# The order of a weight unit's raw halves, and a later, pinned split of the unit two ahead

## The chip, the cores and the metric

One core of a Trainium2 chip runs the whole kernel. The metric is device microseconds of one execution. ACT is ScalarE, DVE is VectorE, POOL is GpSimd, SP is SyncE, which issues nearly all transfers; PE is TensorE.

## The reference

A decoder block on 1024 tokens of width 1024, in fp32: two token mixers side by side, then a squared-ReLU MLP.

```
xn = rmsnorm(x, norm1_g)
qa, ka, va, qr, kr, vr, gr, gate_a, gate_b = columns of xn @ w_in          # 1024 x 12800
o_a = dilated sliding-window attention(qa, ka, va)   # 12 heads of 128, three windows
o_r = chunkwise retention(qr, kr, vr), group norm, times silu(gr)          # 4 heads
y = sigmoid(gate_a) * (o_a @ w_proj_a) + sigmoid(gate_b) * (o_r @ w_proj_b)
x = x + y @ w_out
x = x + square(relu(rmsnorm(x, norm2_g) @ w_up)) @ w_down                  # 1024 x 4096, 4096 x 1024
```

## The kernel before

Every fp32 matrix product is made of three products of rounded parts: each operand is split into a high part (`wh`, `xh`, a copy on ACT to the rounded type) and a low part (`wl`, `xl`, the difference, on DVE). The helper is `split`, lines 351 (ACT) and 352 (DVE); a wide split of 128x1024 is one instruction on each.

Large products go by a Strassen scheme of seven products N1 to N7 instead of eight. A *unit* is 256 output columns of a weight: 1024 x 256 numbers, which arrive as two raw halves of 512 KB, `s[0]` with quarters (x22, x21) and `s[1]` with (x11, x12). From them four pieces are split:

- A: (x11, x12) as it came, for N1 and N2
- D: x22 as it came, for N4; after it four sums (`sums`, line 151, DVE) rewrite both halves in place
- B: the sums in the half of (x11, x12), for N6 and N3
- C: the sums in the half of (x22, x21), for N5 and N7

There are two places for A, two for B, one for C and two half places for D. The raw halves rotate through four places, two to a unit. `Weights` holds the planning: `steps` is the list of splits in order; `pump` carries out the next step when the pieces it overwrites are given back (`before`, from `claim`) and its raw half is loaded; `load` (line 207) issues the next transfer in order of `src` when its place is free. `free` gives a piece back: after N2, N7, N3 and N4. So every transfer and split is written into the program at a point that follows from these rules.

That is the order in which the program is traced. On PE this order is kept. On ACT, DVE and SP a list scheduler of the compiler sets the final order from its own estimates of when each instruction is ready, unless `tc.keep_in_program_order(ins)` pins an instruction behind the one traced before it on its engine. [...]

The order of products around the change, `strassen_order` (line 287): after N1 and N2 of units 0 and 1, unit j brings

```python
order += [(j, "N6"), (j, "N5")] + ([] if late else [(j + 2, "N1")]) + [(j, "N7")]
order += [(j, "N3")]
order += [(j + 2, "N2")] if not late else ...
order += [(j, "N4")]
```

so N1 and N2 of a unit run two units ahead of the rest. A product is 12 matmuls into one bank. `N1`'s negated result goes to a bank in which N6, N7 and N4 accumulate (bank b, tile `ms`, line 419); N6 is copied out (tile `u`, line 424) before N7 may add to the bank, and N5 (line 427) before N3 may add to its own. Lines 429 and 434 finish the results of N7 and N3 on DVE.

The scheme is used twice: in the input stage ("in", 24 units: gates, retention's q and k, and gr), beside which the attention runs; and in the MLP's first half ("up", 16 units). In up, `result` applies relu (line 1219) and square (line 1220), forms the sums of line 1227 that the second half needs, and `put_operand` splits each of seven operands per unit into a tile `hs` (four buffers) and stores it to DRAM (`h_d<-hs`, line 1237). The second half ("dn", w_down) is another Strassen scheme, whose operands come back from DRAM (`xh<-h_d`, `xl<-h_d`, line 1253) and whose weights come as quarters through the same four raw places (sums at line 183).

Of the kernel before, what the change touches and what calls it, by code (L numbers as in the profile page):

```python
# [12 lines left out]
AF = mybir.ActivationFunctionType  # L13
# [6 lines left out]
D = 1024  # L20
# [8 lines left out]
C = 128  # L29
# [8 lines left out]
class Weights:  # L38
# [10 lines left out]
    A, B, C, D = (0, 1), (2, 3), 5, 4  # L49
# [75 lines left out]
    def add_units(self, tag, srcs):  # L125

        base = len(self.src)
        kept = {}
        for s in srcs:
            self.place += [(len(self.src) + i - base) % (self.RAW + 1) for i in range(2)]  # L130
            self.src += [s[0], s[1]]

        def piece(key, buf, r, cols, then=None):
            def step():
                if isinstance(buf, tuple):
                    if not kept:
                        kept["D"] = self.buffer(buf[0])
                    h, l = (x[:, 512 * buf[1]:512 * buf[1] + 512] for x in kept["D"])
                else:
                    h, l = self.buffer(buf)  # L140
                self.split(h, l, self.raw[r][:, cols])
                self.units[key] = h, l
                if then:
                    then()

            self.steps.append((self.claim(buf, key), r, step))

        def sums(r):
            (x22, x21), (x11, x12) = ((self.raw[i][:, 0:512], self.raw[i][:, 512:1024]) for i in (r, r + 1))
            for x, y in ((x22, x21), (x21, x11), (x11, x22), (x12, x11)):  # L150
                self.nc.vector.tensor_tensor(x, x, y, op=OP.add)  # L151

        both = slice(0, 1024)
        for j in range(-1, len(srcs)):
            if j + 1 < len(srcs):
                r = base + 2 * (j + 1)
                piece((tag, j + 1, "A"), self.A[(j + 1) % 2], r + 1, both)
            if j >= 0:
                r = base + 2 * j
                piece((tag, j, "D"), (self.D, j % 2), r, slice(0, 512), lambda r=r: sums(r))  # L160
                piece((tag, j, "B"), self.B[j % 2], r + 1, both, lambda r=r: self.used.add(r + 1))
                piece((tag, j, "C"), self.C, r, both, lambda r=r: self.used.add(r))
        m = len(srcs)
        self.cycle = (0, 1, self.B[m % 2], self.C, self.D, self.B[(m - 1) % 2])
        self.turn = 0
# [135 lines left out]
def hybrid_block(ctx: ExitStack, tc: tile.TileContext, a: dict, out: bass.AP):  # L301
    nc = tc.nc
# [44 lines left out]
    def bcast_row(src):  # L347
        return bass.AP(tensor=src.tensor, offset=src.offset, ap=[[0, P], [1, D]])

    def split(dst_h, dst_l, src):  # L350
        nc.scalar.activation(dst_h, src, AF.Copy)  # L351
        nc.vector.tensor_tensor(dst_l, src, dst_h.bitcast(F), op=OP.subtract)  # L352

    half = const.tile([P, 4], F, name="half")
# [13 lines left out]
    def halves():  # L368
        return (slice(0, 512), slice(512, 1024))


    W = Weights(nc, rawp, wp, split)
    heads = [(slot, g) for slot in range(SLOTS) for g in (1, 2, 0)]
    for u in range(4):
# [134 lines left out]
    with ExitStack() as ph:  # L509
# [11 lines left out]
        def put_transposed(xn, n, q):  # L521
            t = TILES[n]
            pt = tr.tile([P, 4, P], F, name="tr")
            for i in range(4):
                k = 4 * q + i
                nc.tensor.transpose(pt[:, i, :], xn[:, k * P:(k + 1) * P], ident)
            if q == 0 and t >= 4:
                x01[t] = [px.tile([P, 4, P], R, name=f"x01{i}") for i in "hl"]
                split(*x01[t], pt)
                for i in range(2):  # L530
                    nc.sync.dma_start(x01_d[i, :, :, cut(t)], x01[t][i].bitcast(F))
            else:
                split(*(x[:, :, cut(t)] for x in XS[q, t // 4]), pt)
            x = kept[q, t // 4] = px.tile([P, 4, P], F, name=f"x{q}{t // 4}", bufs=1 if t >= 4 else 2)
            nc.scalar.activation(x, pt, AF.Copy)
            if q == 1 and t >= 4:
                x = dict(kept)
                differences(t, x, (("N5", (0, 0), (0, 1), OP.subtract), ("N7", (0, 1), (1, 1), OP.subtract)))
                pipe.at(1, lambda: differences(t, x, (("N6", (1, 1), (0, 0), OP.add),
                                                      ("N4", (1, 0), (1, 1), OP.subtract))))  # L540
# [22 lines left out]
        lo, hi = halves()  # L563
# [631 lines left out]
    with ExitStack() as ph:  # L1195
# [47 lines left out]
        sums = {}  # L1243
# [190 lines left out]
```

## Time and profile before

| | |
|---|---|
| median of 3 runs | 2262.45 us (2255.77 to 2265.8) |
| the profiled execution | 2260.28 us, its span 2258.5 us |
| mean granted clock of PE | 0.993 |
| the input stage with the attention | about 407 to 985 us |
| up | about 1600 to 1940 us |
| down | from there to the end |

How to read the rows: "start, length, engine, line, operation, out<-in" is a row of the timeline, with what ended the engine's idle time before it in brackets. "out<-in" goes by the names of tiles. Rows of waits are "engine, line <- what it waited for: total us, times, longest". Rows by windows give the stretch, its length, busy us and instruction count of PE, PE's weight load, DVE, ACT and POOL, the granted clock, the share of the DMA engines and GB/s.

### The profile page before, as it was taken

The page shows a single profiled execution, that of the slowest core. Times are in us where ns is not written, and L with a number is a line of the kernel's source. Part 1 is how long each engine was busy: PE and PEld are TensorE (multiplying, and loading weights), DVE is VectorE, ACT ScalarE, POOL GpSimd, SP SyncE. Part 2 cuts the span into 40 slices and gives each one's busy share as a digit, 9 for nine tenths or more (in the row PEclk, how much of TensorE's full clock was granted, in tenths as well). Part 3 has the DMA queues.
Part 4 walks back from the last instruction along what each step waited for, and adds up shares of the span by engine and source line. Part 5 has one row for each costly group of instructions (what it writes and reads, how often), then busy time and mean ns, then how long its engine had stood idle before and what let it go on. Part 6 is the DMA issues. An engine that isn't in the chain of part 4 may idle for free.

```text
span 2258.5 us, 28527 instructions
## 1 busy us (share of the span) xinstructions
PE 2189.5 (97%) x10064; PEld 1794.3 (79%) x10064; DVE 1432.1 (63%) x2543; ACT 1103.3 (49%) x1934; POOL 194.1 (9%) x180
## 2 busy tenths in 40 slices
PE   8999999999999999989999999999999999899998
PEld 6788788888888887878888788888787777688887
DVE  6766676455655666557867741544867778676863
ACT  6433453577744477545545522113666667522210
POOL 3314453000000000000000000000000000000002
PEclk9999999999999999999999999999999999999999
DMA  6443534454555445455333583553388779966657
GB/s 197 131 126 112 150 93 123 154 161 146 172 151 166 153 151 162 127 177 153 119 89 115 165 284 126 187 177 134 109 232 229 231 225 284 313 243 249 244 221 172
DMA packets 346559, 392.77 MB, mean 174 GB/s; under 512 B 34737, under 2 KB 271921, under 8 KB 346162
## 3 DMA queue, kind: packets, MB, share of 16 engines
q1 hardware_dynamic: 344114, 386.77, 54.7%
q0 software_dynamic: 2304, 4.20, 1.3%
q8 instruction: 79, 1.29, 0.2%
q14 instruction: 62, 0.51, 0.1%
HBM read 252.39 MB, written 138.51 MB: 173 GB/s over the span
## 4 chain that ended last, share of the span: by engine, by line
PE 71%; DVE 8%; DMA 8%; ACT 6%; issue 4%; POOL 3%; SPq 0%; POOLq 0%; ACTq 0%; DVEq 0%
PE mm L254 41%; PE ms L254 24%; DMA raw<-in_w_up 2%; ACT wh L351 2%; DVE wl L352 2%; DMA h_d<-hs 2%; PE tr L787 1%; PE tr L806 1%; DVE raw L151 1%; DVE hs L352 1%; DMA xl<-h_d 1%; POOL x L547 1%; DMA raw<-in_w_att_q 1%; DVE xl L352 1%; PE tr L645 1%
## 5 line engine op out<-in xcount | busy, mean ns | idle before, releaser
L352 DVE TENSOR_TENSOR wl<-raw,wh 128x1024 fp32r<-128x1024 f32 (+1 forms) x292 | 332.4, 1139 | 231.5 <-ACT wh L351 229.8
L351 ACT ACTIVATE wh<-raw 128x1024 fp32r<-128x1024 f32 (+1 forms) x292 | 287.1, 986 | 321.3 <-PE ms L254 110.5
L254 PE MATMUL mm<-xh,wh 128*128 128x512 f32 x896 | 346.3, 410 | 0.0
L254 PE MATMUL mm<-xl,wh 128*128 128x512 f32 x896 | 329.0, 390 | 1.7 <-DVE xl L352 1.7
L254 PE MATMUL mm<-xh,wl 128*128 128x512 f32 x768 | 300.7, 392 | 0.0
L254 PE MATMUL mm<-wh,xh 128*128 128x512 f32 x736 | 297.8, 405 | 2.3 <-ACT ms L1273 2.3
L254 PE MATMUL mm<-wh,xl 128*128 128x512 f32 x736 | 289.3, 393 | 4.0 <-DMA xl<-h_d 4.0
L254 PE MATMUL mm<-wl,xh 128*128 128x512 f32 x736 | 288.0, 391 | 0.0
L254 PE MATMUL ms<-xh,wh 128*128 128x512 f32 x544 | 228.2, 419 | 15.3 <-ACT u L424 13.4
L254 PE MATMUL ms<-xl,wh 128*128 128x512 f32 x544 | 213.6, 393 | 0.7 <-DVE xl L352 0.7
L254 PE MATMUL ms<-xh,wl 128*128 128x512 f32 x544 | 213.6, 393 | 0.0
L254 PEld LDWEIGHTS mm<-xh,wh 128*128 128x128 f32 x896 | 168.9, 189 | 32.5 <-ACT u L427 0.4
L254 PEld LDWEIGHTS mm<-xl,wh 128*128 128x128 f32 x896 | 169.0, 189 | 31.6 <-DVE xl L352 2.1
L254 PEld LDWEIGHTS mm<-xh,wl 128*128 128x128 f32 x768 | 144.3, 188 | 31.4
L254 PEld LDWEIGHTS mm<-wh,xl 128*128 128x128 f32 x736 | 138.9, 189 | 35.3 <-DMA xl<-h_d 4.9
L254 PEld LDWEIGHTS mm<-wh,xh 128*128 128x128 f32 x736 | 139.2, 189 | 28.8 <-ACT ms L1273 3.2
L254 PEld LDWEIGHTS mm<-wl,xh 128*128 128x128 f32 x736 | 139.5, 189 | 26.0
L254 PE MATMUL ms<-wh,xh 128*128 128x512 f32 x336 | 137.1, 408 | 6.7 <-DVE c L700 4.4
L254 PEld LDWEIGHTS ms<-xh,wh 128*128 128x128 f32 x544 | 102.9, 189 | 40.8 <-ACT u L424 18.5
L254 PE MATMUL ms<-wh,xl 128*128 128x512 f32 x336 | 132.8, 395 | 2.5 <-DVE xl L352 2.5
L254 PE MATMUL ms<-wl,xh 128*128 128x512 f32 x336 | 132.3, 394 | 1.0 <-DVE ss L365 0.8
L254 PEld LDWEIGHTS ms<-xh,wl 128*128 128x128 f32 x544 | 102.7, 189 | 22.5
(282 smaller groups left out, 3809.9 us busy)
## 6 DMA issues: line engine op xcount, KB each, us to landing
h_d<-hs SPq DMA_DIRECT2D x112, 512.0 KB, 5.6
xh<-h_d SPq DMA_DIRECT2D x32, 896.0 KB, 4.9
xl<-h_d SPq DMA_DIRECT2D x32, 896.0 KB, 6.9
raw<-in_w_att_q SPq DMA_DIRECT2D x48, 512.0 KB, 4.3
raw<-in_w_up SPq DMA_DIRECT2D x32, 512.0 KB, 5.0
raw<-in_w_down SPq DMA_DIRECT2D x32, 512.0 KB, 5.2
qk_d<-T SPq DMA_DIRECT2D x48, 256.0 KB, 3.5
raw<-in_w_gate_q SPq DMA_DIRECT2D x16, 512.0 KB, 4.5
```

Of the source, the lines that this page charges most:

```text
L151: self.nc.vector.tensor_tensor(x, x, y, op=OP.add)
L254: self.nc.tensor.matmul(ps, x, y, start=start, stop=stop, skip_group_check=not first)
L351: nc.scalar.activation(dst_h, src, AF.Copy)
L352: nc.vector.tensor_tensor(dst_l, src, dst_h.bitcast(F), op=OP.subtract)
L547: nc.gpsimd.tensor_tensor(x[v], x[v], x[u], op=op)
L645: nc.tensor.transpose(pt[:, i, :], c[:, i * P:(i + 1) * P], ident)
L787: nc.tensor.matmul(sp[:, :w], q[:, e * P:(e + 1) * P], k[:, k0 * P:k0 * P + w], start=True, stop=True)
L806: nc.tensor.matmul(po[:, :DH], st["t"][:, j * P:(j + 1) * P], v[:, k0 + j, :], start=(j == 0), stop=(j == nk - 1))
```

## The change

The two raw halves of a unit change places in the list of transfers: first (x11, x12), then (x22, x21). Everything that names them follows: A and B read the first, D and C the second, so B gives back the first place and C the second. The step of A of unit j + 1 now also waits until A of unit j is given back, which is after N2 of unit j (before, it waited for N2 of unit j - 1 alone, and came right after C). In up, from unit 2 on, the ACT instruction of A's split is pinned in program order. Nothing changes in the arithmetic, the sizes or the number of transfers.

```diff
-            self.src += [s[0], s[1]]
+            self.src += [s[1], s[0]]
 
-        def piece(key, buf, r, cols, then=None):
+        def piece(key, buf, r, cols, then=None, after=(), pinned=False):
...
-                self.split(h, l, self.raw[r][:, cols])
+                self.split(h, l, self.raw[r][:, cols], pinned)
...
-            self.steps.append((self.claim(buf, key), r, step))
+            self.steps.append((self.claim(buf, key).union(after), r, step))
 
         def sums(r):
-            (x22, x21), (x11, x12) = ((self.raw[i][:, 0:512], self.raw[i][:, 512:1024]) for i in (r, r + 1))
+            (x11, x12), (x22, x21) = ((self.raw[i][:, 0:512], self.raw[i][:, 512:1024]) for i in (r, r + 1))
...
-                piece((tag, j + 1, "A"), self.A[(j + 1) % 2], r + 1, both)
+                piece((tag, j + 1, "A"), self.A[(j + 1) % 2], r, both,
+                      after=((tag, j, "A"),) if j > 0 else (), pinned=tag == "up" and j > 0)
             if j >= 0:
                 r = base + 2 * j
-                piece((tag, j, "D"), (self.D, j % 2), r, slice(0, 512), lambda r=r: sums(r))
-                piece((tag, j, "B"), self.B[j % 2], r + 1, both, lambda r=r: self.used.add(r + 1))
-                piece((tag, j, "C"), self.C, r, both, lambda r=r: self.used.add(r))
+                piece((tag, j, "D"), (self.D, j % 2), r + 1, slice(0, 512), lambda r=r: sums(r))
+                piece((tag, j, "B"), self.B[j % 2], r, both, lambda r=r: self.used.add(r))
+                piece((tag, j, "C"), self.C, r + 1, both, lambda r=r: self.used.add(r + 1))
...
-    def split(dst_h, dst_l, src):
-        nc.scalar.activation(dst_h, src, AF.Copy)
+    def split(dst_h, dst_l, src, pinned=False):
+        hi = nc.scalar.activation(dst_h, src, AF.Copy)
+        if pinned:
+            tc.keep_in_program_order(hi)
         nc.vector.tensor_tensor(dst_l, src, dst_h.bitcast(F), op=OP.subtract)
```

## The prediction, made before the changed kernel was run

> **What bounds the kernel now.** First the busy times of the page: is one engine the bound, and how much of the span could a change of order give back at all?
>
> ```profile
> span 2258.5 us, 28527 instructions
> PE 2189.5 (97%) x10064; PEld 1794.3 (79%) x10064; DVE 1432.1 (63%) x2543; ACT 1103.3 (49%) x1934; POOL 194.1 (9%) x180
> ```
>
> PE is busy 97%, so a change that leaves PE's work alone can win at most its 69 us of idleness, and only the part that lies in the units. Next, the waits of PE alone in the up stage (1660 to 1930 us) and in the input stage (407 to 985 us), and then those of ACT in up.
>
> ```profile
> PE ms L254 <- ACT u L424: 12.6, 10, 2.2
> ...
> PE ms L254 <- ACT u L424: 0.8, 1, 0.8
> ...
> ACT wh L351 <- DMA raw<-in_w_up: 52.0, 12, 5.7
> ACT wh L351 <- DVE raw L151: 18.7, 14, 2.0
> ACT hs L351 <- DMA h_d<-hs: 9.5, 15, 1.5
> ```
>
> The columns are total us, times, longest. In up PE waits ten times for the copy of N6 at line 424 (it frees the bank into which N7 accumulates); in the input stage once. ACT itself sits 52 us behind splits whose raw half has not landed. That the second makes the first has to be seen in time: ACT over one unit, with SP's weight loads and PE's N7 at the two ends.
>
> ```profile
> 1699.31 0.62 ACT L351 ACTIVATE wh<-raw 128x512 fp32r<-128x512 f32 x1
> 1700.98 0.50 PE L254 MATMUL ms<-xh,wh 128*128 128x512 f32 x1 [1.00 <-ACT u L424]
> 1703.88 0.39 PE L254 MATMUL mm<-xh,wh 128*128 128x512 f32 x1
> 1704.06 1.06 ACT L351 ACTIVATE wh<-raw 128x1024 fp32r<-128x1024 f32 x1 [1.96 <-DVE raw L151]
> 1706.07 1.04 ACT L351 ACTIVATE wh<-raw 128x1024 fp32r<-128x1024 f32 x1
> 1706.41 0.35 SPq L207 DMA_DIRECT2D raw<-in_w_up  x1
> 1706.90 0.68 DVE L429 TENSOR_TENSOR u<-ms,u 128x512 f32<-128x512 f32 x1
> 1710.70 1.06 ACT L351 ACTIVATE wh<-raw 128x1024 fp32r<-128x1024 f32 x1 [3.59 <-DMA raw<-in_w_up]
> 1711.66 0.61 ACT L1219 ACTIVATE u<-u 128x512 f32<-128x512 f32 x1
> 1711.79 1.23 DVE L352 TENSOR_TENSOR wl<-raw,wh 128x1024 fp32r<-128x1024 f32 x1 [3.07 <-ACT wh L351]
> 1718.13 0.64 ACT L351 ACTIVATE hs<-q 128x512 fp32r<-128x512 f32 x1 [0.23 <-DMA h_d<-hs]
> 1720.19 0.59 ACT L424 ACTIVATE u<-ms 128x512 f32<-128x512 f32 x1
> 1720.83 0.50 PE L254 MATMUL ms<-xh,wh 128*128 128x512 f32 x1 [0.47 <-ACT u L424]
> ```
>
> The narrow split at 1699.31 is D of the next unit; the three wide ones are B and C of the next unit and A of the third unit on (called A(j+3) in slot j, a slot being the stretch from one N7 to the next). A's half is asked for at 1706.41, when B's split has freed its place, and lands at 1710.70. ACT takes its queue in order: the relu at 1711.66, whose operand L429 had ready at 1706.90 + 0.68 = 1707.6, and all behind it run about 4 us late, the copy of line 424 with them. It ends when N7 should long have begun. So in up PE is bound by an engine that is itself blocked in front of a transfer.
>
> **The stretch that can be won.** From N7 of unit 3 to N7 of unit 15:
>
> ```profile
> 1680.79 0.39 PE L254 MATMUL ms<-xh,wh 128*128 128x512 f32 x1
> 1919.11 0.39 PE L254 MATMUL ms<-xh,wh 128*128 128x512 f32 x1
> 1681.00:1919.00 238.00, 225.34 (x972) 182.38 (x971) 180.01 (x250) 160.39 (x260) 0.00 (x0) 0.99 0.84 244
> 1618.39 5.44 PE mm L254 x24
> ```
>
> 972 matmuls are 81 products of 12. An undisturbed product takes 5.44 / 2 = 2.72 us (the chain's row), so 81 need 220.3 us; they took 1919.11 - 1680.79 = 238.3. The excess is 18.0 us: 12.6 of waits, some 0.35 at each restart (1700.98 to the next product at 1703.88 is 2.90, and a copy's drain before it), and one stretch at half clock:
>
> ```profile
> 1864.08 0.50 PE L254 MATMUL ms<-xh,wh 128*128 128x512 f32 x1 [2.22 <-ACT u L424]
> 1864.80:1868.30 3.50, 3.50 (x11) 2.67 (x10) 2.97 (x5) 2.18 (x4) 0.00 (x0) 0.51 1.04 282
> ```
>
> After the 2.22 us wait the granted clock is 0.51 for 3.5 us, which costs about 3.5 x 0.49 = 1.7 us, part of the 18.0.
>
> **The change part by part.**
>
> Order of the halves. No transfer is added or dropped and none changes its size. The first half of a unit now takes the place that B frees, the second the one that C frees. In up this is already how the transfers go (1706.41 follows B's split, the next weight load follows C's), so A's half lands when it did, about 9.7 us after N7's start (1710.70 - 1700.98): price 0. In SP's queue it keeps its neighbours. One place differs: the first quarter of the down weights now takes the place that B of unit 14 frees instead of C's.
>
> ```profile
> 1889.43 0.96 SPq L207 DMA_DIRECT2D raw<-in_w_down  x1
> 1891.76 0.35 SPq L207 DMA_DIRECT2D raw<-in_w_down  x1
> 1898.06 1.06 ACT L351 ACTIVATE wh<-raw 128x1024 fp32r<-128x1024 f32 x1 [1.85 <-DMA raw<-in_w_down]
> 1902.36 0.50 PE L254 MATMUL ms<-xh,wh 128*128 128x512 f32 x1 [1.74 <-ACT u L424]
> ```
>
> It moves 1891.76 - 1889.43 = 2.3 us ahead, more than the 1.85 that ACT waits; that wait fed the 1.74 of PE behind it. I take it as gone; if not, 1.9 us of the 18.0 stay.
>
> A's split later and, in up, pinned. Its step now waits for N2 of the unit before, so in slot j it is traced after N2(j+2), and its ACT half keeps its place behind the hs split of that N2's result (the row at 1718.13, 17.1 us after N7). Without the 3.59 of waiting and A's own 1 us the relu at 1711.66 starts at about 1707.6, so the chain behind it moves up by some 4 us: that hs split ends at 1718.77 - 4.1 = 1714.7. A then takes 1.06 on ACT and 1.23 on DVE: done at about 1717.0 by these rows, and N1(j+3) is due at 1700.98 + 6 x 2.72 = 1717.3. That is tight, but DVE and ACT drift forward with it: the D split at 1699.31, and the four sums between it and B at 1704.06, begin some 3 us sooner too, and with them B and L429. I take the slack as 0.3 to 3 us and the wait at N1 as 0. What ACT is left with in up is 18.7 us of waits on the sums and 9.5 on the stores of hs, both inside its idle time (160.4 busy of 238). Line 424 of N6, which ends 5.4 us before N7 is due, then comes out at 1720.19 - 3 or better, ahead of N7 at 1700.98 + 19.04 = 1720.0. Gain in this stretch: 18.0, less 0.5 for stray waits = 17.5.
>
> The cover is thin where up begins. A(2) is pinned too, and there the hs split of N2(1)'s result is late for another reason: relu, square and split all wait for the last operand tiles of the stage before.
>
> ```profile
> 1611.96 1.05 ACT L351 ACTIVATE wh<-raw 128x1024 fp32r<-128x1024 f32 x1
> 1616.17 0.63 ACT L351 ACTIVATE xh<-x 128x512 fp32r<-128x512 f32 x1 [1.79 <-DVE x L1144]
> 1616.70 1.07 ACT L1219 ACTIVATE q<-mm 128x512 f32<-128x512 f32 x2
> 1621.72 0.61 ACT L351 ACTIVATE hs<-q 128x512 fp32r<-128x512 f32 x1
> 1620.94 0.39 PE L254 MATMUL mm<-xh,wh 128*128 128x512 f32 x1
> ```
>
> A(2) was split at 1611.96; it now follows the hs split, which ends at 1622.3. Plus 1.06 and 1.23 that is 1624.6, against N1(2) due at 1620.94: a new wait of 3.7 us, once. Since A's own 2.3 us of work no longer stand ahead of those splits, they may come some 2 us sooner: 1.5 is the lower end. I take 2.5. **The clock's rule.** The row at 1864.08 shows a half clock after 2.22 us of idleness, while 1.74 at 1902.36 left it alone. [...]
>
> In the input stage the split is later but not pinned, and no wait of PE there hangs on a split (0.8 us on line 424 in all). A's split ran a whole slot before its N1; it now has N4, N6 and N5 between, 3 x 2.72 = 8.2 us for 2.3 us of work on an ACT that is busy 49% over the span. I take 0; bounds: the 0.8 gained, 3 lost. The turn into down (1930 to 1985 us) has PE waits of its own:
>
> ```profile
> PE mm L254 <- DMA xl<-h_d: 7.8, 3, 3.8
> PE mm L254 <- ACT ms L1273: 2.2, 1, 2.2
> PE ms L254 <- ACT Y L1280: 1.0, 1, 1.0
> ```
>
> These 11 us hang mostly on loads of h_d, which the change neither adds to nor moves within the turn; I take 0, with 3 either way.
>
> **Sum.** -17.5 + 2.5 + 0 + 0 = -15.0 us. The profiled execution took 2260.28 (its span is 2258.5), which is 2.2 below the median of 2262.45. 2260.3 - 15 = 2245; set against the median 2247. I say 2246. About 0.5%, 11 us, is what a measurement of this kernel can tell from no change.
>
> **The rivals.**
> Line 424 stays late (0.13). ACT's other waits, 18.7 on the sums and 9.5 on the stores, could fill the hole that A leaves, since hs splits would come while the weights are still landing. For it: 4 hs buffers, DMA at 0.84 in this stretch. Against: 28 us of waits beside 78 us of ACT idleness. Half the excess would stay: 18 / 2 - 2.5 = 6.5 gained, about 2255.
> A comes late at N1 (0.16). The pin sets it behind a store (4 us), and the slack by rows was only 0.3 us. With 0.8 us of waiting in each of 13 units, 10.4 us go back: about 2257.
> The same, but more, so that it turns slower (0.08). The hs split of N2 waits for the store four before it. If stores that now share the queues with the weight loads take 3 us longer than at 1718.13, N1 waits 2.7 us in 13 units, 35 us against 15: 2260 + 20 = 2280. It decides at 15 / 13 = 1.2 us a unit.
> The change does not do what it says, A still before its data: excluded in up by the pin, since 1718 is far behind 1710.7.
>
> **How the numbers follow.** The forecast has 0.63: its own range is 2240 to 2251 (start of up 1.5 to 5.4, turn +-3, A at N1 0 to 2). Its top is at the 0.5% line, so 0.03 of it counts as the same. Faster 0.60, same 0.03 + 0.13 + 0.16 = 0.32, slower 0.08. For 8 in 10 the range takes in the two middle cases: 2239 to 2259.
>
> **What the profile after would show.** ACT's wait on the raw halves of up falls from 52 us to under 5; the PE wait on line 424 in up from 12.6 to under 2; N7 follows N7 after 19.04 to 19.2 us instead of some 20.3; no half clock inside up; one PE wait of 1.5 to 4 us, on a wl, at the third N1 of up. The input stage keeps its length within 3 us. The prediction is wrong if mm waits on wl (line 352) repeat in every unit, or if hs waits for h_d grow beyond 20 us.

## The result and the profile after

The changed kernel takes 2249.15 us (median; 2244.55 to 2251.35) against 2262.45 before: 13.3 us less, ratio 0.9933 with a 95% interval of 0.9921 to 0.9946. The forecast was 2246, within 2239 to 2259. The profiled execution took 2249.58 us, its span is 2247.8, which is 10.7 below the span before. In the changed file all lines of interest have moved by 1 to 3: matmul 255, split 352 and 355, copies of N6 and N5 427 and 430, relu 1222, square 1223, sums 1230.

The page of the changed kernel first:

```profile
span 2247.8 us, 28538 instructions
...
PE 2189.5 (97%) x10064; PEld 1797.2 (80%) x10064; DVE 1433.9 (64%) x2543; ACT 1108.9 (49%) x1936; POOL 195.6 (9%) x180
```

PE is busy for the same 2189.5 us as before, so the 10.7 us by which the spans differ are idleness of PE: 69.0 us became 58.3. (A stretch at a lower clock counts as busy, 3.41 us of 3.41 at 0.50 in one window below; where that matters it is said there.) Next the waits of PE from 1600 to 1920 us, which also takes in the start of up, and those of ACT from 1640 to 1920 us:

```profile
PE tr L1127 <- DVE x L1147: 2.8, 1, 2.8
PE mm L255 <- DVE xl L355: 1.7, 1, 1.7
PE mm L255 <- ACT wh L352: 1.2, 1, 1.2
PE ms L255 <- ACT u L427: 1.0, 1, 1.0
PE mm L255 <- DVE wl L355: 0.5, 1, 0.5
...
ACT hs L352 <- DVE q L1230: 23.5, 28, 2.2
ACT u L1222 <- DVE u L437: 18.1, 14, 1.4
ACT wh L352 <- PE ms L255: 15.6, 12, 1.3
ACT u L430 <- PE mm L255: 11.3, 13, 0.9
ACT hs L352 <- DMA h_d<-hs: 2.8, 3, 1.0
...
ACT wh L352 <- DVE raw L151: 0.2, 1, 0.2
```

The row of 52.0 us in which ACT stood in front of a raw half of up has no successor at all, and the ten PE waits for the copy of N6 are one, of 1.0. ACT still waits a lot (23.5 us on DVE's sums, 18.1 on the finished N3), but PE does not stand still for it: the windows below have no idle moment of PE from 1640 to 1900 us. Two rows of PE are new, 1.2 and 0.5, one time each: the third N1 of up. The first two rows, 2.8 and 1.7, were there before as well (2.80 and 1.71).

One unit in the timeline of the changed kernel: N7, the loads, ACT's queue up to the copy of N6, N7 again.

```profile
1804.10 0.39 PE L255 MATMUL ms<-xh,wh 128*128 128x512 f32 x1
1806.29 3.19 SPq L208 DMA_DIRECT2D raw<-in_w_up  x2
1815.12 1.16 ACT L352 ACTIVATE hs<-q 128x512 fp32r<-128x512 f32 x2 [0.32 <-DVE q L1230]
1816.17 1.05 ACT L352 ACTIVATE wh<-raw 128x1024 fp32r<-128x1024 f32 x1
1817.25 1.83 DVE L355 TENSOR_TENSOR wl<-raw,wh 128x1024 fp32r<-128x1024 f32 x2 [0.18 <-ACT wh L352]
1818.64 0.58 ACT L427 ACTIVATE u<-ms 128x512 f32<-128x512 f32 x1
1823.14 0.39 PE L255 MATMUL ms<-xh,wh 128*128 128x512 f32 x1
```

A's split (1816.17) now stands behind the hs split of N2's result, 9.9 us after its half was asked for (the first load of the row at 1806.29), and does not wait. The copy of N6 ends at 1819.2, 3.9 us ahead of N7; before, it ended at the moment N7 began. N7 follows N7 after 19.04 us. N1 of the unit two ahead is due at 1804.10 + 6 x 2.72 = 1820.4; A's high part is done at 1817.2, its low part (the first of the two in the DVE row) at about 1818.5, so A has some 2 us of slack.

The same number of matmuls of up, 1149, in two windows, before and then after (columns: length, then busy us and count of PE, PEld, DVE, ACT and POOL, then granted clock, DMA share, GB/s):

```profile
1631.00:1909.00 278.00, 265.34 (x1149) 215.49 (x1148) 207.92 (x291) 185.08 (x301) 0.00 (x0) 0.99 0.83 238
1640.00:1900.00 260.00, 260.00 (x1149) 215.38 (x1148) 211.82 (x292) 189.69 (x304) 0.00 (x0) 1.00 0.90 253
```

278 became 260, and in the second row PE has no idle moment and the full clock. That is more than the whole gain; the difference is given back at the start of up:

```profile
1605.00:1631.00 26.00, 22.47 (x101) 17.79 (x100) 20.70 (x31) 17.30 (x28) 0.00 (x0) 1.00 0.29 90
1610.00:1640.00 30.00, 25.49 (x101) 19.88 (x100) 19.85 (x30) 15.92 (x27) 0.00 (x0) 0.89 0.27 84
```

Again before and then after, 101 matmuls each: 26 became 30, at a granted clock of 0.89. The rows behind it, of the changed kernel:

```profile
1621.04 0.63 ACT L352 ACTIVATE xh<-x 128x512 fp32r<-128x512 f32 x1 [1.79 <-DVE x L1147]
1623.33 1.06 ACT L1222 ACTIVATE q<-mm 128x512 f32<-128x512 f32 x2
1625.32 1.15 ACT L352 ACTIVATE hs<-q 128x512 fp32r<-128x512 f32 x2
1626.36 1.05 ACT L352 ACTIVATE wh<-raw 128x1024 fp32r<-128x1024 f32 x1
1627.46 0.50 PE L255 MATMUL mm<-xh,wh 128*128 128x512 f32 x1 [1.19 <-ACT wh L352]
1628.72 0.50 PE L255 MATMUL mm<-xh,wl 128*128 128x512 f32 x1 [0.53 <-DVE wl L355]
1626.39:1629.81 3.42, 1.82 (x7) 1.21 (x8) 2.11 (x3) 2.00 (x4) 0.00 (x0) 1.00 0.91 293
1629.81:1633.22 3.41, 3.41 (x10) 2.64 (x9) 0.00 (x0) 0.58 (x1) 0.00 (x0) 0.50 0.50 141
```

A(2) waits for relu, square and split of an N2 result that the stage before held up. N1 waits 1.19 for the high part and 0.53 for the low part, and then runs at a granted clock of 0.50 for 3.41 us, which costs another 3.41 x 0.50 = 1.7. The mean of 0.89 holds a second such stretch, from 1616.15 on, behind the wait of 2.8 us that both kernels have. Before, that wait left the clock at 1.00; the section on the hardware has the rows of both, and that the difference goes with the execution and not with the change is the author's reading of them. By the times of the same matmuls it costs 0.4 of the 4.1 below; without it PE waits 0.67 us there for another operand.

The ledger of the two profiled spans, by the times of the same PE instructions (after less before; the parts of the kernel are those of the table further down): first stage +5.2, input stage +0.3, from there to up -0.6, start of up +4.1, from the window's start to N7 of unit 14 -17.9, N7 of unit 15 +1.1, the turn and down -2.9; together -10.7.

### The profile page after: what moved, and what is told of

The parts are those of the page before. It is cut to its first block, busy times and chain, and to the rows that moved or that the text cites. A ratio compares the mean times of both kernels' runs of the same rounds, so it can differ in the third digit from the quotient of the medians.

```text
span 2247.8 us, 28538 instructions
## 1 busy us (share of the span) xinstructions
PE 2189.5 (97%) x10064; PEld 1797.2 (80%) x10064; DVE 1433.9 (64%) x2543; ACT 1108.9 (49%) x1936; POOL 195.6 (9%) x180
## 4 chain that ended last, share of the span: by engine, by line
PE 78%; DVE 6%; DMA 5%; ACT 5%; issue 3%; POOL 2%; SPq 0%; POOLq 0%; ACTq 0%; DVEq 0%
PE mm L255 45%; PE ms L255 27%; DVE wl L355 1%; PE tr L790 1%; PE tr L809 1%; ACT wh L352 1%; DMA xl<-h_d 1%; DVE xl L355 1%; PE tr L648 1%; DMA h_d<-hs 1%; POOL x L550 1%; PE ms L931 1%; DVE raw L151 1%; PE tr L802 1%; PE tr L987 1%
```

## The experiments

Each is an edit of the changed kernel unless it says otherwise; every ratio is against the kernel before, timed on the same chip. Theory: the gain is the transfer in front of which ACT stood, so only what moves A's split behind it counts, and neither the order of halves nor the pin alone. The main rivals: the order of halves carries part of it; or fewer splits in ACT's queue ahead of the copy do, whatever the transfer.

**The order of halves alone** (A queued as before, no pin).

```
-                      after=((tag, j, "A"),) if j > 0 else (), pinned=tag == "up" and j > 0)
+                      after=(), pinned=False)
```

> The changed order of the two raw halves alone; the split of A stays where it was in the kernel before. Theory (the gain is the transfer in front of which ScalarE stands, and that is set by where the split of A is queued): ScalarE still waits some 50 us in 12 units of up for raw from in_w_up, TensorE still waits 10 to 14 us for the copy of N6, and the time is 2262 plus or minus 3, the ratio 0.998 to 1.002. Rival (the order of halves carries part of the gain by itself): 2252 to 2257, and the wait for raw well under 40 us.

2263.55 us, ratio 1.0004 (0.9994 to 1.0014). Its waits of PE and of ACT from 1660 to 1930 us:

```profile
PE ms L255 <- ACT u L427: 13.5, 9, 3.5
...
ACT wh L352 <- DMA raw<-in_w_up: 49.1, 11, 6.1
```

The kernel before has 12.6 us in 10 waits and 47.6 us in 11 waits in this window (the 52.0 in 12 of the prediction begins earlier). Nothing of the stall has gone. The order of halves by itself is worth nothing.

**Later and pinned, with the old order of halves** (the three places of the diff that name the halves turned back).

> The later and pinned split of A alone; the raw halves stay in the order (x22, x21), then (x11, x12). The theory (in up N7 waits because ACT stands in front of a transfer, and moving A's split behind that transfer cures it) expects the whole gain: 2249 +-3 us, ratio to before about 0.994, ACT's wait on the raw halves of up under 5 us, PE's wait on the copy of N6 in up under 2 us. Rival: the order of the halves carries a part, since A's half would be asked for later; then 2254 to 2262 us and some of the 52 us of ACT's wait stay.

2244.84 us, ratio 0.9924 (0.991 to 0.9938). From 1660 to 1930 us no wait of PE for the copy of N6 and none of ACT for raw from in_w_up is left. The later split carries the gain without the new order. The time lies below the 2246 to 2252 that was expected; the table at the end of this section shows where the rest may come from.

**Later, not pinned.**

```
-                      after=((tag, j, "A"),) if j > 0 else (), pinned=tag == "up" and j > 0)
+                      after=((tag, j, "A"),) if j > 0 else (), pinned=False)
```

> The change without the pin: halves in the new order, A's step later in the list, its place on ACT left to the scheduler. The theory expects that the scheduler puts A right behind C again, in front of the transfer: 2262 +-3 us, ACT's wait on the raw halves of up about 50 us, PE's wait on the copy of N6 about 12 us. Rival: the later step is enough and the pin does nothing: 2249 +-3 us, both waits gone.

**Pinned, not later.**

```
-                      after=((tag, j, "A"),) if j > 0 else (), pinned=tag == "up" and j > 0)
+                      after=(), pinned=tag == "up" and j > 0)
```

> The change without the later step: halves in the new order, A pinned on ACT in up, but behind C, where it is traced without the later step. The theory expects no gain: 2262 +-3 us, ACT's wait on the raw halves of up 45 to 55 us, PE's wait on the copy of N6 in up 11 to 14 us. Rival: any pin helps since it stops the scheduler from other moves: below 2255 us.

2260.64 us, ratio 1.0002 (0.999 to 1.0014), and 2265.75, ratio 1.0018 (1.0007 to 1.0029). The same two rows, 1660 to 1930 us, of the kernel without the pin and then of the one that is not later:

```profile
PE ms L255 <- ACT u L427: 13.3, 10, 3.8
...
ACT wh L352 <- DMA raw<-in_w_up: 46.2, 11, 5.6
```

```profile
PE ms L255 <- ACT u L427: 11.5, 9, 3.3
...
ACT wh L352 <- DMA raw<-in_w_up: 46.8, 11, 5.2
```

The second lies 0.75 us above the range that was expected for it. Both parts, the later step and the pin, are needed. Traced later but free, the split is set back in front of its transfer by the compiler's scheduler; pinned behind C, it stands there by order.

**A's half already there.** ACT's queue as in the pinned, not later kernel but for one place, and A of units 2 and up is split from the raw half of the unit before, which has long landed:

```
-                piece((tag, j + 1, "A"), self.A[(j + 1) % 2], r, both,
-                      after=((tag, j, "A"),) if j > 0 else (), pinned=tag == "up" and j > 0)
+                piece((tag, j + 1, "A"), self.A[(j + 1) % 2], r - 2 if tag == "up" and j > 0 else r, both,
+                      after=(), pinned=tag == "up" and j > 0)
```

> As the one with the pin behind C, on ACT in the same order from unit 3 on, but from unit 2 of up on A is split from the half of the unit before, which has long landed; the same transfers run, and N1 and N2 of those units use the wrong weights. So A keeps its place in ACT's queue and only its wait for the transfer goes. The theory expects the whole gain of the stretch, 15 to 18 us, without the wait at the third N1: 2244 to 2248 us, ACT's wait on raw halves of up under 3 us, PE's wait on the copy of N6 under 2 us. Rival: it is A's microsecond of work in front of the relu that makes the copy late, not the wait: then PE's wait stays above 8 us and the time at 2258 to 2264 us.

2244.42 us, ratio 0.9929 (0.9916 to 0.9942). Its waits from 1640 to 1920 us:

```profile
PE ms L255 <- ACT u L427: 0.3, 1, 0.3
...
ACT u L427 <- PE ms L255: 9.1, 13, 0.7
```

No row of ACT for raw from in_w_up is left. This settles the cause. A's split stands as early as before, with its 1.06 us of ACT work ahead of relu and copies, and the stall is gone, because the wait for the transfer is. The copy of N6 now even waits for PE (9.1 us in 13 units) instead of PE for it. It was the blocked queue, not ACT's load or the number of splits ahead of the copy.

**One product later still**, in up from the third unit: A waits for N4 of the unit two before, behind that product's split.

```
-                      after=((tag, j, "A"),) if j > 0 else (), pinned=tag == "up" and j > 0)
+                      after=((tag, j - 2, "D") if tag == "up" and j > 1 else (tag, j, "A"),) if j > 0 else (), pinned=tag == "up" and j > 0)
```

> The changed kernel with the split of A of the unit two ahead one product later still, behind the split of hs of the third product of the unit instead of the second. Theory (about 2 us of slack at N1 in the changed kernel, while one product is some 2.7 to 6 us of the unit): the weights of N1 come too late by 2 to 5 us in each of some 12 units of up, TensorE waits 25 to 60 us for wh or wl of N1, and the time is 2275 to 2310. Rival (the slack at N1 is larger than read, since the two products ahead of it give way): under 10 us of such waits and a time within 5 us of 2249.

2302.93 us, ratio 1.0182 (1.0164 to 1.02). Waits of PE from 1640 to 1960 us; one unit from N7 to N7; and the stretch with its two waits, with the one behind it:

```profile
PE mm L255 <- ACT wh L352: 23.6, 12, 2.7
PE mm L255 <- DVE wl L355: 8.5, 12, 0.7
...
1804.39 0.39 PE L255 MATMUL ms<-xh,wh 128*128 128x512 f32 x1
1814.39 0.50 PE L255 MATMUL mm<-xh,wh 128*128 128x512 f32 x1 [1.68 <-ACT wh L352]
1815.85 0.50 PE L255 MATMUL mm<-xh,wl 128*128 128x512 f32 x1 [0.72 <-DVE wl L355]
1828.03 0.39 PE L255 MATMUL ms<-xh,wh 128*128 128x512 f32 x1
...
1812.91:1816.32 3.41, 1.21 (x4) 0.73 (x5) 3.38 (x5) 2.86 (x4) 0.00 (x0) 1.00 1.01 281
1816.32:1819.73 3.41, 3.41 (x10) 2.65 (x9) 0.61 (x1) 0.00 (x0) 0.00 (x0) 0.50 1.05 262
```

The prediction's rival "A comes late at N1" is real, one product away. N7 follows N7 after 23.64 us instead of 19.04. Of these 4.60 the waits are 1.68 + 0.72 = 2.40; the rest, 2.2, is the half clock that follows (3.41 x 0.50 = 1.7) and the restart. In twelve units that is 55, and the kernel is 53.8 us above the changed one. So a wait of this shape cost nearly twice what the rows of waits show.

**The first A of up left free** (pinned from unit 3 on).

```
-                      after=((tag, j, "A"),) if j > 0 else (), pinned=tag == "up" and j > 0)
+                      after=((tag, j, "A"),) if j > 0 else (), pinned=tag == "up" and j > 1)
```

> The change with A of unit 2 in up not pinned (pinned from unit 3 on). The theory expects that the scheduler puts A(2) where it was before, ahead of the operand splits' end, so that the wait of 1.7 us at the third N1 of up goes and with it the half clock behind it: 2 to 4 us less than the changed kernel, 2244 to 2248 us. Rival: the place was needed by B(1) and the operands, so that N6 of unit 1 or the first N6 waits instead: no gain.

2245.36 us, ratio 0.9924 (0.9909 to 0.994). The changed kernel, timed again beside it, took 2248.58, ratio 0.9934 (0.9914 to 0.9955): 3.2 more. The intervals overlap, so the time alone does not show the gain. The profile does: the two waits at the third N1 are gone, and up is 297.2 us long, against 302.1 and 301.6 in the two profiles of the changed kernel. Run again, the changed kernel was also expected to have a shorter first stage than in its first profile, up to the length of before; it has not (412.7 us against 412.3, and 407.1 before).

**Later in up alone** (the input stage planned as before).

```
-                      after=((tag, j, "A"),) if j > 0 else (), pinned=tag == "up" and j > 0)
+                      after=((tag, j, "A"),) if tag == "up" and j > 0 else (), pinned=tag == "up" and j > 0)
```

> The change with the later step in up alone; in the input stage A's step comes right after C as before, only with the new order of the halves. The theory expects no difference to the changed kernel: +-1.5 us, the input stage 578 us as in both profiles so far. Rival: the later split in the input stage brought or cost something: a difference of 3 us or more, in the stretch from 407 to 985 us.

2248.74 us, ratio 0.9937 (0.9923 to 0.9951): the same as the changed kernel, and its input stage takes 568.8 us against 568.3. With the new order of halves, the later split does nothing in the input stage.

**The two together: old order of halves, later, first A free.**

> Old order of the halves, A later and pinned from unit 3 of up on (A of unit 2 free). If the two small losses add, 2 to 4 us at the start of up and those of the new order (the changed kernel stood 4 us above the one with the old order, in different runs), this is the fastest: 2241 to 2244 us. Rival: those 4 us were chance, then as the kernel with the new order and A(2) free, 2244 to 2248 us.

2241.49 us, ratio 0.9899 (0.9886 to 0.9913), the fastest of all and below both kernels. Its PE waits from 1600 to 1930 us hold no copy of N6 and no split at all:

```profile
PE mm L255 <- DMA xl<-h_d: 4.1, 1, 4.1
PE tr L1127 <- DVE x L1147: 2.8, 1, 2.8
PE ms L255 <- ACT Y L1283: 0.6, 1, 0.6
```

**That kernel with the later split in up alone**, to find where its extra microseconds come from.

> The kernel with the old order of halves, the later split of A, and the first unit's A(2) left free (2241.49 us), with the later split in up alone: the input stage plans the split of A as before the change. Theory (the input stage is some 4 us shorter in those runs since the later split acts there too, with the old order): its input stage is back at 567 to 569 us, and the time is 2244 to 2247. Rival (the 4 us come from something else, such as the code after it): the input stage stays near 563.5 and the time near 2241.5.

2244.19 us, ratio 0.9922 (0.9907 to 0.9937). Lengths of the stages in the profiled executions in us (first stage: up to the first product of the input stage's units; input: from there to the first matmul of the retention; up: from the last transpose before it to its last product). The last column counts the periods of 3.41 us at half clock in the first stage:

| kernel | first stage | input stage | up | half-clock periods in the first stage |
|---|---|---|---|---|
| before | 407.1 | 568.0 | 314.6 | 1 |
| after | 412.3 | 568.3 | 302.1 | 4 |
| order of halves alone | 410.3 | 568.8 | 318.3 | 2 |
| after, run again | 412.7 | 570.4 | 301.6 | 4 |
| later, pinned, old order | 412.8 | 563.9 | 299.0 | 3 |
| later, not pinned | 408.7 | 567.0 | 316.8 | 2 |
| pinned, not later | 412.2 | 567.5 | 316.4 | 4 |
| A's half already there | 410.4 | 568.6 | 298.3 | 3 |
| one product later still | 408.8 | 568.2 | 358.7 | 2 |
| first A free | 413.2 | 568.7 | 297.2 | 4 |
| later in up alone | 414.4 | 568.8 | 299.8 | 4 |
| old order, first A free | 411.1 | 563.5 | 296.5 | 3 |
| that one, later in up alone | 411.8 | 569.4 | 296.6 | 3 |

The input stage is 3 to 7 us shorter in the two kernels that have the old order and the later split there, and in none that lacks one of them: by these profiles, a gain that the changed kernel with its new order does not have. It was seen in one profile of each; the medians 2241.49 and 2244.19 point the same way, but the intervals of their ratios overlap. How it comes about is open. The input windows show where to look, not why (with the later split there, then in up alone):

```profile
411.10:974.60 563.50, 554.17 (x2686) 456.55 (x2685) 324.55 (x830) 351.59 (x630) 0.00 (x0) 1.00 0.51 156
411.80:981.20 569.40, 557.37 (x2687) 458.92 (x2685) 325.54 (x830) 357.49 (x635) 0.00 (x0) 0.99 0.51 154
```

PE is idle 9.3 us instead of 12.0 and busy 3.2 less. The 3.2 are not the schedule's: the second kernel has 6.83 us at half clock from 852.0 us on, which cost 3.4, and the first has none there. ACT has 630 instructions instead of 635 and is busy 5.9 us less. Four of the five fewer are loads of ACT's function tables, 79 against 83 in its groups of instructions, 1.28 us each. The other kernel with the short input stage also has 79, and all the rest have 83 or 85. So another order of splits in ACT's queue goes with another number of table loads. Whether these loads shorten the stage was not tried.

## Why the prediction was right

- *What bounds up*: right. ACT blocked in front of a raw transfer makes the copy of N6 late and PE with it. The kernel in which A's half has already landed removes the stall without moving the split, and the later split with the old order removes it too.
- *The stretch, 17.5 gained*: 17.9 measured from the start of the window to N7 of unit 14, and N7 follows N7 after 19.04. The 0.5 kept back for stray waits became one wait of 0.99 at N7 of unit 15, with 1.1 in the ledger, so that 16.8 are gained over the whole stretch. Ahead of that copy ACT waits 0.87 and 0.95 us for stores of hs and 0.33 for a quarter of the down weights. That is the first rival's mechanism (stores in ACT's way), seen at one unit only.
- *Order of the halves, 0*: right, by the kernel with the order alone (1.0004). One step inside it was not. The 1.74 at N7 of unit 14 was to go because the first quarter of the down weights is asked for sooner. ACT's split of that quarter, with the order alone and then with the later split and the old order:

```profile
1904.25 1.06 ACT L352 ACTIVATE wh<-raw 128x1024 fp32r<-128x1024 f32 x1 [2.71 <-DMA raw<-in_w_down]
1883.24 1.06 ACT L352 ACTIVATE wh<-raw 128x1024 fp32r<-128x1024 f32 x1 [0.24 <-DMA raw<-in_w_down]
```

The order alone leaves the wait (2.71 us, 1.85 before), and the waits of PE at units 13 and 14, 1.67 and 1.74, become one of 3.50 at unit 13. With the old order and the later split ACT waits 0.24 and PE not at all. So it was the later, pinned split that removed this wait; that it went as forecast was luck. What the sum did not have is the 4 us of the input stage, which by the profiles above the later split brings with the old order only.

- *A at N1, slack 0.3 to 3 us, wait 0*: right; about 2 us, and one product more is too much.
- *Start of up, 2.5*: 4.1 in the profiled pair. The wait itself was sized right: up takes 299.0 us (old order) and 299.8 (new order) in two kernels that have it and no half clock behind it, and with the first A free 296.5 and 297.2, which is 2.5 and 2.6 less. What was mis-sized is the half clock behind it, 1.7, for which the sum has no term. The sum lets the clock stay up behind the new wait, which was the author's estimate: before the change the granted clock was 0.51 for 3.5 us behind a wait of 2.22, and in the changed kernel it was 0.50 for 3.41 us behind 1.19 + 0.53. It is not a fixed price either: of the five profiles with this wait (about 1.2 to 1.5 us and 0.5) it follows in two, both of the changed kernel. With the 1.7 the sum is -15.0 + 1.7 = -13.3, and the medians differ by 13.3; so close a match is partly chance, since the last two points below are left out of it.
- *Input stage, 0*: right, +0.3. *First stage*: no term, +5.2 in the profiled pair. ACT, DVE and SP take the same instructions in the same order through the first 407 us. The table shows what differs: the stage takes 407.1 us with one half-clock period, 408.7 to 410.3 with two, 410.4 to 412.8 with three and 412.2 to 414.4 with four. Three periods more than before, at 1.7 each, come to 5.1 of the 5.2. Other kernels have two to four with the same instructions up to there, so the number goes with the execution, as far as one profile of before can say.
- *Turn into down, 0 +-3*: -2.9 with down, inside the bound; the stall for xl from h_d is shorter there, 5.7 us against 7.8. The cause was not tried.

Of the signs listed for the profile after, all were seen except two: half clock did come inside up (at its start), and the new wait came on wh first and wl second.

## What to carry to other kernels

ACT's wait for a transfer (3.59 us in the unit that the prediction shows) was paid by all that stood behind it in its queue, some 4 us: if a split waits like that, ask which small copy behind it frees a bank that TensorE needs, and queue the split behind work whose operands are there by then. Tracing it later was not enough where the scheduler could move it back (ratio 1.0002), nor was pinning it in an early place (1.0018); and pin only where the work ahead of it is on time, since at a stage's first units that work may itself be late. Look for the slack at the consumer before moving further: here it was 2 us, and one product more turned 13 us of gain into a loss of 41.

## What the runs showed of the hardware

The granted clock fell to 0.50 behind gaps of about 2 us, and the length of a gap did not decide alone. In the kernel with A one product later, PE waits 1.68 us, issues two matmuls, waits 0.72, and the granted clock is 0.50 from 1816.32 to 1819.73 us. A window with eleven such units:

```profile
1660.00:1930.00 270.00, 241.32 (x960) 190.85 (x960) 172.93 (x242) 159.61 (x255) 0.00 (x0) 0.93 0.71 200
```

A mean of 0.93 over 270 us is what eleven units with 3.4 us at half clock each make: 11 x 3.4 x 0.5 / 270 = 0.07. Before the change, the same stood behind a single wait of 2.22 us (0.51 from 1864.80 to 1868.30 us), and not behind a single one of 1.74 (1.00 from 1902.42 to 1905.83). The wait of 2.8 us at the start of up, which PE has in both kernels (2.80 and 2.79), was followed by half clock in one of the two profiles. Two stretches around it before the change, then two after:

```profile
1605.47:1608.88 3.41, 2.02 (x11) 1.33 (x9) 3.41 (x7) 1.63 (x3) 0.00 (x0) 1.00 0.39 148
1608.88:1612.29 3.41, 2.01 (x11) 1.77 (x12) 3.41 (x7) 2.57 (x5) 0.00 (x0) 1.00 0.03 5
1612.74:1616.15 3.41, 1.00 (x7) 0.94 (x8) 3.41 (x7) 2.07 (x4) 0.00 (x0) 1.00 0.00 0
1616.15:1619.57 3.42, 3.42 (x10) 2.68 (x9) 3.42 (x7) 1.99 (x4) 0.00 (x0) 0.50 0.02 5
```

The stretches are cut on a grid of 3.41 us on which the changes of the clock lie in these two traces: all of them lie a whole number of 3.41 us apart, and each half-clock stretch but the last of the kernel is 3.41 or 6.83 us long. Before, the wait falls on two stretches, PE is idle 1.4 us in each, and the clock stays at 1.00 in both and in the next. After, 2.4 us of it fall into one stretch, and the next runs at 0.50. Counted over all stretches of the two traces from 16 us to the last change of the clock: from full clock it fell behind every one with 1.94 us or more of PE's idleness, behind none with less than 1.60, and between these both occur: behind 1.60 it fell (after, from 1626.39 us on), behind 1.87 it did not (before, from 1963.87 us on). The changes do not lie at the same places of the work in the two executions, as the rows show: behind the same wait of 2.8 us one has 3.42 us at 0.50, by these numbers at most 3.42 x 0.50 = 1.7 us, and the other none.

The first stages of the two executions, with the same work, differ in this too: one period of 3.41 us at half clock before, four after (1.00 and 0.98 in mean granted clock, 407.1 and 412.3 us long). So 5 us of difference between two single profiles, ahead of the first instruction that the change reaches, should not be put down to a change.
